# A two-layer decoder trunk on one core: one rank for all work, half-size weight parts in the mixers, and two of four weight sums of an FFN block made by an ACT copy and an accumulating DMA

## The chip, the cores and the metric

The kernel runs on one core of a Trainium2 chip. The metric is device time in microseconds (us) of one execution; lower is better. The engines are named as in the profile: PE (matrix multiplications; PEld is its weight load), DVE, ACT, POOL, and SP, which issues most loads.

## The reference, cut to what matters

The reference runs 256 positions of width 2048 through two layers in float32. Layer 0 mixes with a state-space part and a latent attention, layer 1 with a stick-breaking attention; each mixer is followed by a gated feed-forward network (FFN) of hidden width 5632.

```python
for layer in range(DEPTH):                      # DEPTH = 2
    h = rms_norm(x, mix_norm[layer])
    mix = ssd_mla_mixer(h, ...) if layer % 2 == 0 else stick_breaking_mixer(h, w_qkv[o], w_out_odd[o])
    x = x + mix
    x = x + swiglu_ffn(rms_norm(x, ffn_norm[layer]), w_gate[layer], w_up[layer], w_down[layer])
return rms_norm(x, final_norm)

def swiglu_ffn(h, w_gate, w_up, w_down):
    return (jax.nn.silu(h @ w_gate) * (h @ w_up)) @ w_down
```

## The kernel before, in words

**Products.** Every float32 weight is split into two parts that PE takes at full rate: `split` (L247) lets ACT copy the tile `w` into a rounded high part `wh` (L249), and DVE subtracts it from `w` to give the low part `wl` (L250). The activations are split the same way. A product is then three matmuls: high by high, low by high, high by low. Weights are loaded by SP in tiles of 128 partitions x 4 x 512 floats (1 MB), called `w`. There are four of them in turn during an FFN and three elsewhere; `wh` and `wl` have three each during an FFN and two elsewhere (`wtile`, L102). The fourth and the third lie in a shared pool that `region` (L88) opens and closes with each stage.

**Projections.** `project` (L333) computes 512 output columns for both halves of the positions: for each of 16 (or 8, or 12) k tiles of 128 rows it issues six matmuls (L340 to L342), so that one weight tile of four k feeds 24 matmuls. `load_split` (L300) loads and splits the weights. After each k tile `tick` (L81) moves a count of units on and lets waiting pieces of side work (transposes, attention, norms) issue their instructions.

**FFN blocks.** `ffn` (L550) goes through 11 blocks of 512 hidden columns in groups of 2, 2, 2, 2 and 3. A block is `pair` (L467): it computes gate and up together. For the first half of the contraction it takes seven products of 512 x 512 in place of eight, after the manner of Strassen: of the tiles b11 (gate), b12 (up), b22 (up) and b21 (gate) it forms t1 = b11 + b12, t2 = t1 + b22, t4 = t2 + b21 and t3 = b12 + b22 on DVE (`wadd`, L461, run at L464), splits seven tiles (b11, b22, t1, b21, t2, t4, t3, in that order of use) and runs 12 matmuls for each (L493, L494, L498). The second half is done plainly: four tiles called `cl`, 24 matmuls for each (L526 to L528). At its end `left` and `right` (L558, L559, L564, L566) make the hidden block h, which is transposed by PE within the next block, two units after its start. After each group a down projection by `project` follows: 8 or 12 weight tiles, each pair of output tiles added to the residual x by `add_residual` (L390, run on DVE at L395). PE transposes the new x for the next stage (L259, L413).

**What sets the order.** PE's instructions stand in the order in which the code is written. On every other engine and queue a scheduler puts the instructions in an order of its own when the program is built: of what is ready it takes the one with the lowest priority number. At run time each engine keeps strictly to that order. Weight work has numbers that count up from 100000 (`self.wprio`, +1000 for a projection's tile, +100 for each step of a block); side work that names nothing has 10000000, that is, after all weight work that is ready; what is marked `URGENT` has 50000.

Of the kernel before, what the change touches and what calls it, by code (L numbers as in the profile page):

```python
# [27 lines left out]
class Trunk:  # L28
# [6 lines left out]
    def __init__(self, ctx, tc, ins, out):  # L35
        self.tc, self.nc, self.i, self.out = tc, tc.nc, ins, out
        ec = ctx.enter_context
        self.cp = ec(tc.tile_pool(name="const", bufs=1))
        self.wp = ec(tc.tile_pool(name="weights", bufs=4))
        self.ap = ec(tc.tile_pool(name="acts", bufs=42))  # L40
        self.sp = ec(tc.tile_pool(name="small", bufs=2))
        ps = bass.MemoryType.PSUM
        self.pacc = ec(tc.tile_pool(name="pacc", bufs=1, space=ps))
        self.ptr = ec(tc.tile_pool(name="ptr", bufs=4, space=ps))
        self.dp = ec(tc.tile_pool(name="scratch", bufs=1, space=bass.MemoryType.DRAM))
        self.shared, self.shared_kind = None, None
# [3 lines left out]
        self.n, self.wn = 0, {}  # L50
        self.now, self.tasks = 0, []
        self.wprio = 100000
        tc.cur_priority = 10000000

    @contextmanager
    def priority(self, at):

        keep, self.tc.cur_priority = self.tc.cur_priority, at
        yield
        self.tc.cur_priority = keep  # L60


    def spawn(self, gen):
# [16 lines left out]

    def tick(self):  # L81
        self.now += 1
        ready = [t for t in self.tasks if t["wake"] <= self.now]
        for t in ready[:2]:
            if not t["done"]:
                self.advance(t)

    def region(self, kind):  # L88

        if self.shared is not None:  # L90
            self.shared.__exit__(None, None, None)
        self.shared, self.shared_kind = None, kind
        if kind:
            bufs = 20 if kind == "acts" else 2
            self.shared = self.tc.tile_pool(name=f"shared_{kind}", bufs=bufs, reuse_waits="tile")
# [12 lines left out]

    def whtile(self):
        return self.wtile("wh", F32R, 3, 2)  # L110

    def wltile(self):
        return self.wtile("wl", F32R, 3, 2)

    def wsum(self):
        return self.xp.tile([P, 4, 512], F32, name=self.nm("wsum"), tag="wsum", bufs=2)
# [25 lines left out]
    def constants(self):  # L142
# [4 lines left out]
        with self.priority(0):  # L147
            nc.sync.dma_start(rows_m, i["mix_norm"].rearrange("l (k p) -> (l k) p", p=P))
        for j in range(4):
            with self.priority(self.wprio + 1000 * j - 500):  # L150
                nc.sync.dma_start(self.xres[:, :, j * 512:(j + 1) * 512],
                                  i["x"][0, :, j * 512:(j + 1) * 512].rearrange("(t p) d -> p t d", p=P))
        with self.priority(self.wprio + 3500):
            self.small_loads(rows_a, rows_b)
        with self.priority(self.wprio + 6500):
# [144 lines left out]
    def load_split(self, view, nk, n):  # L300

        nc = self.nc
        for k0 in range(0, nk, 4):
            k1 = min(nk, k0 + 4)
            res = []
            with self.priority(self.wprio):
                self.wprio += 1000
                w = self.wtile()
                for dst, src in view(w, k0, k1):
                    nc.sync.dma_start(dst, src)  # L310
                order = ExitStack()
                for ins in self.first if self.wprio <= 105000 else ():
                    order.enter_context(self.tc.issue_after(ins))
                wh, wl = self.whtile(), self.wltile()
                step = 1 if self.wprio < 102000 else 2 if self.wprio < 106000 else k1 - k0
                for c in range(0, k1 - k0, step):
                    d = c + step
                    self.split(wh[:, c:d, :n], wl[:, c:d, :n], w[:, c:d, :n])
                order.close()
                for k in range(k0, k1):  # L320
                    res.append((wh[:, k - k0, :n], wl[:, k - k0, :n]))
            yield from res

    @staticmethod
# [65 lines left out]
    def add_residual(self, ps, j, scale=None):  # L390
        nc, x = self.nc, self.xres
        for t in range(2):
            xs = x[:, t, j * 512:(j + 1) * 512]
            if scale is None:
                nc.vector.tensor_tensor(xs, ps[t], xs, op=ALU.add)  # L395
            else:
                nc.vector.scalar_tensor_tensor(xs, ps[t], scale[:, t:t + 1], xs, op0=ALU.mult, op1=ALU.add)


    URGENT = 50000  # L400
# [42 lines left out]
            res.append((hi, lo))  # L443
        return res

    def wload(self, view, k0):
        w = self.wtile()
        with self.priority(self.wprio):
            self.wprio += 100
# [4 lines left out]
    def wsplit(self, w):  # L454
        wh, wl = self.whtile(), self.wltile()
        with self.priority(self.wprio):
            self.wprio += 100
            self.split(wh, wl, w)
        return wh, wl

    def wadd(self, o, p, q):  # L461
        with self.priority(self.wprio):
            self.wprio += 100
            self.nc.vector.tensor_tensor(o, p, q, op=ALU.add)  # L464
        return o

    def pair(self, st, xT, va, vb, left, right):  # L467
# [11 lines left out]
        w22 = self.wsplit(b22)  # L479
        wt1 = self.wsplit(t1)  # L480
        t4 = self.wadd(self.wsum(), t2, b21)
        w21 = self.wsplit(b21)
        wt2, wt4, wt3 = self.wsplit(t2), self.wsplit(t4), self.wsplit(t3)
        self.join(st["xT"][0][0])
        self.join(st["xT"][1][0])
        z, p3, p2, p4 = self.banks
# [42 lines left out]
        for half in range(2):  # L529
            k0, last = 8 + 4 * half, half == 1  # L530
            for side in range(2):
                wh, wl = self.wsplit(cl[half][side])
# [593 lines left out]
```

## Time and profile before

| | before |
|---|---|
| median of 3 runs | 2513.11 us (2512.77 to 2513.15) |
| profiled execution, its own time | 2512.09 us |
| its span in the trace | 2510.4 us |
| mean granted PE clock | 0.991 |
| PE, DVE, ACT, POOL busy | 98%, 68%, 52%, 5% of the span |
| read from HBM | 450.85 MB, 180 GB/s over the span |

The profiled execution is 1.7 us longer than its span, and 1.0 us under the median. The first mixer fills the first 641 us of the span, FFN 0 runs to about 1320 us, the second mixer to 1779 us, FFN 1 to the end. Busy shares are averages over these stages; a wait counts only where it ends last.

### The profile page before, as it was taken

The numbers are of one execution on the slowest core, as the hardware profiler recorded it, in microseconds if no ns is written. First come the engines' busy times: TensorE is split into PE (matmuls) and PEld (weight loads), VectorE is DVE, ScalarE is ACT, GpSimd is POOL, SyncE is SP. The second block draws the span as 40 slices with busy tenths as digits, with TensorE's granted clock in tenths as the row PEclk, the third lists the DMA queues.
The fourth block names the chain that finished last, engine by engine and source line by source line (L and its number), as shares of the span: only waits on it lengthen the run. The fifth ranks groups of instructions, "written<-read, shape, count | busy, mean of one in ns | idle before, by whom it ended". The sixth has DMA issues, their size and how long they took to land.

```text
span 2510.4 us, 27612 instructions
## 1 busy us (share of the span) xinstructions
PE 2454.1 (98%) x11176; PEld 2008.4 (80%) x11176; DVE 1714.3 (68%) x1476; ACT 1298.1 (52%) x1266; POOL 130.9 (5%) x164
## 2 busy tenths in 40 slices
PE   8999999999899999999999999999899999999998
PEld 7788877788688888888878787778688888888876
DVE  5775455456778778787965444445787878787874
ACT  6655555434554545454544545554554545454553
POOL 1231121000000000000000000000000000000001
PEclk9999999999899999999999999999999999999999
DMA  7654553355555556565554454445555656565653
GB/s 234 194 176 159 178 157 111 126 193 185 182 197 199 194 196 206 184 203 185 204 190 143 166 172 160 151 155 173 181 200 184 217 172 215 170 231 168 235 188 114
DMA packets 257824, 454.78 MB, mean 181 GB/s; under 512 B 20716, under 2 KB 45424, under 8 KB 257696
## 3 DMA queue, kind: packets, MB, share of 16 engines
q1 hardware_dynamic: 255168, 446.48, 53.1%
q0 software_dynamic: 1952, 5.48, 0.6%
q8 instruction: 88, 1.44, 0.2%
q10 hardware_dynamic: 576, 1.05, 0.1%
q14 instruction: 40, 0.33, 0.0%
HBM read 450.85 MB, written 2.13 MB: 180 GB/s over the span
## 4 chain that ended last, share of the span: by engine, by line
PE 56%; issue 39%; ACT 2%; DVE 1%; POOL 0%; DMA 0%; SPq 0%; POOLq 0%; ACTq 0%; DVEq 0%
PE acc L341 11%; PE acc L340 11%; PE acc L342 11%; PE acc L527 3%; PE acc L526 3%; PE acc L528 3%; PE acc L493 3%; PE acc L494 3%; PE acc L498 3%; PE tr L259 1%; ACT wh L249 1%; DVE wl L250 1%; PE at L1049 1%; PE at L978 1%; PE at L1048 0%
## 5 line engine op out<-in xcount | busy, mean ns | idle before, releaser
L250 DVE TENSOR_TENSOR wl<-w,wh 128x2048 fp32r<-128x2048 f32 (+2 forms) x431 | 966.3, 2250 | 578.3 <-ACT wh L249 569.5
L249 ACT CAST wh<-w 128x2048 fp32r<-128x2048 f32 (+2 forms) x431 | 807.3, 1875 | 732.5 <-PE acc L342 414.8
L340 PE MATMUL acc<-wh,s 128*128 128x512 f32 (+1 forms) x1728 | 692.2, 401 | 3.3 <-ACT wh L249 3.3
L341 PE MATMUL acc<-wl,s 128*128 128x512 f32 (+1 forms) x1728 | 673.6, 390 | 7.0 <-DVE wl L250 6.9
L342 PE MATMUL acc<-wh,s 128*128 128x512 f32 (+1 forms) x1728 | 674.2, 390 | 0.0
L341 PEld LDWEIGHTS acc<-wl,s 128*128 128x128 f32 x1728 | 326.2, 189 | 74.4 <-DVE wl L250 10.3
L342 PEld LDWEIGHTS acc<-wh,s 128*128 128x128 f32 x1728 | 325.3, 188 | 70.2
L340 PEld LDWEIGHTS acc<-wh,s 128*128 128x128 f32 x1728 | 325.9, 189 | 67.6 <-ACT wh L249 4.1
L528 PE MATMUL acc<-wl,s 128*128 128x512 f32 x704 | 275.3, 391 | 0.0
L527 PE MATMUL acc<-wh,s 128*128 128x512 f32 x704 | 275.2, 391 | 0.0
L526 PE MATMUL acc<-wh,s 128*128 128x512 f32 x704 | 275.2, 391 | 0.0
L493 PE MATMUL acc<-wh,s 128*128 128x512 f32 x616 | 246.4, 400 | 0.0
L494 PE MATMUL acc<-wh,s 128*128 128x512 f32 x616 | 242.4, 393 | 0.0
L249 ACT CAST wh<-wsum 128x2048 fp32r<-128x2048 f32 x66 | 125.9, 1910 | 84.6 <-PE acc L527 35.7
L498 PE MATMUL acc<-wl,s 128*128 128x512 f32 x616 | 166.1, 391 | 0.0
L250 DVE TENSOR_TENSOR wl<-wsum,wh 128x2048 fp32r<-128x2048 f32 x66 | 150.6, 2285 | 13.8 <-ACT wh L249 13.8
L527 PEld LDWEIGHTS acc<-wh,s 128*128 128x128 f32 x704 | 132.2, 188 | 29.1
L526 PEld LDWEIGHTS acc<-wh,s 128*128 128x128 f32 x704 | 132.2, 188 | 29.0
L528 PEld LDWEIGHTS acc<-wl,s 128*128 128x128 f32 x704 | 132.1, 188 | 29.0
L493 PEld LDWEIGHTS acc<-wh,s 128*128 128x128 f32 x616 | 116.9, 190 | 25.6
L494 PEld LDWEIGHTS acc<-wh,s 128*128 128x128 f32 x616 | 117.0, 190 | 24.3
L498 PEld LDWEIGHTS acc<-wl,s 128*128 128x128 f32 x616 | 115.8, 188 | 25.7
(246 smaller groups left out, 2063.3 us busy)
## 6 DMA issues: line engine op xcount, KB each, us to landing
w<-in_w_gate_dram SPq DMA_DIRECT2D x88, 1024.0 KB, 5.1
w<-in_w_up_dram SPq DMA_DIRECT2D x88, 1024.0 KB, 5.1
w<-in_w_down_dram SPq DMA_DIRECT2D x88, 1024.0 KB, 5.0
w<-in_w_qkv_dram SPq DMA_DIRECT2D x48, 1024.0 KB, 5.0
w<-in_w_in_dram SPq DMA_DIRECT2D x47, 1024.0 KB, 5.2
w<-in_w_out_even_dram SPq DMA_DIRECT2D x32, 1024.0 KB, 4.9
w<-in_w_out_odd_dram SPq DMA_DIRECT2D x16, 1024.0 KB, 5.0
w<-in_w_ukv_dram SPq DMA_DIRECT2D x32, 256.0 KB, 4.1
```

Source lines behind the costliest of these rows:

```text
L249: nc.scalar.copy(hi, src)
L250: nc.vector.tensor_tensor(lo, src, hi.bitcast(F32), op=ALU.subtract)
L259: self.nc.tensor.transpose(pt[:, k, t * P:(t + 1) * P], src(t, 2 * k2 + k), self.ident)
L340: nc.tensor.matmul(ps[t], hi[:, ts], wh, start=k == 0, stop=False)
L341: nc.tensor.matmul(ps[t], hi[:, ts], wl, start=False, stop=False)
L342: nc.tensor.matmul(ps[t], lo[:, ts], wh, start=False, stop=k == nk - 1)
L493: mm(ps, hi[:, k], wh[:, k], start=start and k == 0, stop=False, skip_group_check=True)
L494: mm(ps, lo[:, k], wh[:, k], start=False, stop=False, skip_group_check=True)
L498: mm(ps, hi[:, k], wl[:, k], start=False, stop=k == 3, skip_group_check=True)
L526: mm(ps, hi, wh, start=False, stop=False, skip_group_check=True)
L527: mm(ps, lo, wh, start=False, stop=False, skip_group_check=True)
L528: mm(ps, hi, wl, start=False, stop=stop, skip_group_check=True)
```

## The change

1. **One rank.** `due(units)` gives a priority of 100000 + 250 times the unit at which something is needed. Weights get `due(0)` at the point of the program that uses them, and within a block 0, 2, 4 ... 26 units for its steps. Side work gets `due(4)` at each `tick`, so that it stands four units behind the weights of the same place and no longer behind all of them. `add_residual` becomes `URGENT`.
2. **Half-size parts in the mixers.** `wh` and `wl` come from `part`: in the mixers four buffers of two k tiles in place of two of four, in the FFNs three of four as before; all of them lie in the shared pool now. A 1 MB tile `w` is split there by two pairs of instructions.
3. **Two sums by DMA.** b12 is no longer loaded as a tile. t1 is made by an ACT copy of b11 into `wsum` and a DMA on POOL's queue that loads b12 and adds it to what stands there; t3 is made the same way from b22 in a `w` tile. t2 and t4 stay on DVE. A block loads seven tiles on SP and two by accumulating DMAs on POOL, where it loaded eight on SP.

```diff
+    def due(self, units):
+        return self.base + 250 * (self.now + units)
...
     def tick(self):
         self.now += 1
+        self.tc.cur_priority = self.due(self.SLACK)
...
-    def wtile(self, tag="w", dt=F32, bufs=4, own=3):
-        n = self.wn[tag] = self.wn.get(tag, 0) + 1
-        if self.shared_kind == "sums" and n % bufs == 0:
-            return self.xp.tile([P, 4, 512], dt, name=self.nm(tag), tag=tag, bufs=1)
-        return self.wp.tile([P, 4, 512], dt, name=self.nm(tag), tag=tag, bufs=own)
...
+    def wtile(self):
+        self.wn += 1
+        pool, bufs = (self.xp, 1) if self.shared_kind == "sums" and self.wn % 4 == 0 else (self.wp, 3)
+        return pool.tile([P, 4, 512], F32, name=self.nm("w"), tag="w", bufs=bufs)
+    def part(self, tag):
+        nk, bufs = (2, 4) if self.shared_kind == "acts" else (4, 3)
+        return self.xp.tile([P, nk, 512], F32R, name=self.nm(tag), tag=tag, bufs=bufs)
...
-            with self.priority(self.wprio):
-                self.wprio += 1000
+            with self.priority(self.due(0)):
                 w = self.wtile()
...
+                np = 2 if self.shared_kind == "acts" else 4
+                for a in range(k0, k1, np):
+                    b = min(k1, a + np)
+                    wh, wl = self.part("wh"), self.part("wl")
...
             xs = x[:, t, j * 512:(j + 1) * 512]
-            if scale is None:
-                nc.vector.tensor_tensor(xs, ps[t], xs, op=ALU.add)
...
+            with self.priority(self.URGENT):
+                if scale is None:
+                    nc.vector.tensor_tensor(xs, ps[t], xs, op=ALU.add)
...
+    def wcopy_add(self, o, p, view, k0, at):
+        with self.priority(self.due(at)):
+            self.nc.scalar.copy(o, p)
+            for dst, src in view(o, k0, k0 + 4):
+                self.nc.gpsimd.dma_start(dst, src, accum_op=ALU.add)
+        return o
...
-        b11, b12 = self.wload(va, 0), self.wload(vb, 0)
-        b22, b21 = self.wload(vb, 4), self.wload(va, 4)
-        cl = [(self.wload(va, 8), self.wload(vb, 8)), (self.wload(va, 12), self.wload(vb, 12))]
-        t1 = self.wadd(self.wsum(), b11, b12)
-        w11 = self.wsplit(b11)
-        t2 = self.wadd(self.wsum(), t1, b22)
-        t3 = self.wadd(b12, b12, b22)
...
+        b11, b22, b21 = (self.wload(*a) for a in ((va, 0, 0), (vb, 4, 2), (va, 4, 6)))
+        t1 = self.wcopy_add(self.wsum(), b11, vb, 0, 0)
+        t3 = self.wcopy_add(self.wtile(), b22, vb, 0, 2)
+        cl = [(self.wload(va, 8, 14), self.wload(vb, 8, 18)), (self.wload(va, 12, 22), self.wload(vb, 12, 26))]
+        w11, w22 = self.wsplit(b11, 0), self.wsplit(b22, 2)
+        wt1 = self.wsplit(t1, 4)
+        w21 = self.wsplit(b21, 6)
+        t2 = self.wadd(self.wsum(), t1, b22, 8)
+        wt2 = self.wsplit(t2, 8)
+        wt4 = self.wsplit(self.wadd(self.wsum(), t2, b21, 10), 10)
+        wt3 = self.wsplit(t3, 12)
```

PE's order is the same, instruction by instruction. The changed file has lines of its own: L250 becomes L255, L395 becomes L403, L464 becomes L477, L558 becomes L570, L566 becomes L578, the ACT copy is L470 and the accumulating DMA L472. Three places show how the order moves on the other engines.

**First place: DVE where the first mixer ends and FFN 0 begins.** `xres` is the residual x; the two rows on it add the last projection's two results, after which PE transposes x. Before, where `wsum_920` is t1, `wsum_923` t2, `w_913` t3 and `wsum_928` t4:

```order
L250 TENSOR_TENSOR wl_922_5152<-w_912_5133,wh_921_5151 128x2048
L395 TENSOR_TENSOR xres_80<-acc_878_4941,xres_80 128x512
L464 TENSOR_TENSOR wsum_920_5149<-w_912_5133,w_913_5135 128x2048
L250 TENSOR_TENSOR wl_925_5159<-w_914_5137,wh_924_5158 128x2048
L464 TENSOR_TENSOR wsum_923_5155<-wsum_920_5149,w_914_5137 128x2048
L464 TENSOR_TENSOR w_913_5135<-w_913_5135,w_914_5137 128x2048
L250 TENSOR_TENSOR wl_927_5163<-wsum_920_5149,wh_926_5162 128x2048
L395 TENSOR_TENSOR xres_80<-acc_879_4942,xres_80 128x512
```

The same place in the change, where `wsum_1107` is t1 (copied by ACT, then added to by the DMA), `w_1105` is b22 and `wsum_1121` is t2:

```order
L403 TENSOR_TENSOR xres_80<-acc_1062_5299,xres_80 128x512
L403 TENSOR_TENSOR xres_80<-acc_1063_5300,xres_80 128x512
L255 TENSOR_TENSOR wl_1114_5528<-w_1104_5507,wh_1113_5527 128x2048
L477 TENSOR_TENSOR wsum_1121_5543<-wsum_1107_5513,w_1105_5509 128x2048
L255 TENSOR_TENSOR wl_1116_5532<-w_1105_5509,wh_1115_5531 128x2048
L255 TENSOR_TENSOR wl_1118_5536<-wsum_1107_5513,wh_1117_5535 128x2048
L275 SCALAR_TENSOR_TENSOR s2_1094_5475<-tr_1092_5469,va_142,s2_1093_5474 128x256 x2
```

The five weight operations between the two adds are gone from there. The sum t2, which reads what the DMA writes, now stands ahead of the low part of b22, the tile of the second product.

**Second place: DVE across the seam of two neighbouring blocks in FFN 0.** The first row is the last `cl` tile of a block, the first L477 the next block's t2; L570, L576 and L578 finish the first block's h. The change:

```order
L255 TENSOR_TENSOR wl_1144_5746<-w_1112_5525,wh_1143_5745 128x2048
L477 TENSOR_TENSOR wsum_1162_5812<-wsum_1148_5782,w_1146_5778 128x2048
L570 TENSOR_TENSOR s2_1133_5575<-acc_1131_5561,s2_1133_5575 128x512
L255 TENSOR_TENSOR wl_1155_5797<-w_1145_5776,wh_1154_5796 128x2048
L570 TENSOR_TENSOR s2_1136_5654<-acc_1132_5562,s2_1136_5654 128x512
L255 TENSOR_TENSOR wl_1157_5801<-w_1146_5778,wh_1156_5800 128x2048
L578 SCALAR_TENSOR_TENSOR s2_1136_5654<-acc_1129_5559,rstd_1103_5499,s2_1136_5654 128x512
L576 TENSOR_TENSOR s2_1135_5628<-acc_1130_5560,s2_1135_5628 128x512
L578 SCALAR_TENSOR_TENSOR s2_1133_5575<-s2_1135_5628,rstd_1103_5499,s2_1133_5575 128x512
L255 TENSOR_TENSOR wl_1159_5805<-wsum_1148_5782,wh_1158_5804 128x2048
```

Before, three sums (L464) stood among these rows; now one does, and everything below it waits for the DMA that makes t1.

**Third place: ACT in the second mixer, at the logarithms of a group's attention.** L699 before and L711 in the change are the logarithms, with the load of their table ahead; `wh_1810` before and `wh_2050`, `wh_2052` in the change are the high part of the same weight tile. Before:

```order
L249 CAST wh_1798_10768<-w_1797_10766 128x2048
L688 ACTIVATE s2_1784_10704<-at_1783_10701 128x384
L691 ACTIVATE s2_1785_10705<-s2_1784_10704 128x384
L692 ACTIVATE s2_1785_10705<-s2_1785_10705 128x384
L699 ACT_TABLE_LOAD
L699 ACTIVATE s2_1776_10654<-s2_1776_10654 128x384
L699 ACTIVATE s2_1779_10671<-s2_1779_10671 128x384
L699 ACTIVATE s2_1782_10688<-s2_1782_10688 128x384
L249 CAST s2_1789_10738<-s2_1776_10654 128x384
L699 ACTIVATE s2_1785_10705<-s2_1785_10705 128x384
L249 CAST s2_1791_10744<-s2_1779_10671 128x384
L249 CAST wh_1810_10815<-w_1809_10813 128x2048
```

The change:

```order
L711 ACT_TABLE_LOAD
L711 ACTIVATE s2_2012_11127<-s2_2012_11127 128x384
L711 ACTIVATE s2_2015_11144<-s2_2015_11144 128x384
L711 ACTIVATE s2_2018_11161<-s2_2018_11161 128x384
L254 CAST s2_2027_11215<-s2_2012_11127 128x384
L711 ACTIVATE s2_2021_11178<-s2_2021_11178 128x384
L254 CAST s2_2029_11221<-s2_2015_11144 128x384
L254 CAST wh_2050_11296<-w_2049_11294 128x1024
L254 CAST s2_2031_11227<-s2_2018_11161 128x384
L254 CAST wh_2052_11300<-w_2049_11294 128x1024
```

The weight tile stands in the same place, but its first half is a row of half the size.

More of the change, by code (lines that the diff above doesn't have):

```diff
@@ L93, in region @@
         if kind:
-            bufs = 20 if kind == "acts" else 2
-            self.shared = self.tc.tile_pool(name=f"shared_{kind}", bufs=bufs, reuse_waits="tile")
+            self.shared = self.tc.tile_pool(name=f"shared_{kind}", bufs=2, reuse_waits="tile")
             self.xp = self.shared.__enter__()
@@ L311, in load_split @@
                 order = ExitStack()
-                for ins in self.first if self.wprio <= 105000 else ():
+                for ins in self.first if self.now < 16 else ():
                     order.enter_context(self.tc.issue_after(ins))
[L314 to L318, printed above, removed]
+                np = 2 if self.shared_kind == "acts" else 4
+                for a in range(k0, k1, np):
+                    b = min(k1, a + np)
+                    wh, wl = self.part("wh"), self.part("wl")
+                    step = 1 if self.now < 4 else np
+                    for c in range(0, b - a, step):
+                        d = min(c + step, b - a)
+                        self.split(wh[:, c:d, :n], wl[:, c:d, :n], w[:, a - k0 + c:a - k0 + d, :n])
+                    for k in range(a, b):
+                        res.append((wh[:, k - a, :n], wl[:, k - a, :n]))
                 order.close()
-                for k in range(k0, k1):
-                    res.append((wh[:, k - k0, :n], wl[:, k - k0, :n]))
             yield from res
@@ L452, in wload, with wsplit, wadd @@
         return w
[L454 to L457, printed above, removed]
+    def wsplit(self, w, at):
+        wh, wl = self.part("wh"), self.part("wl")
+        with self.priority(self.due(at)):
             self.split(wh, wl, w)
         return wh, wl
[L461 to L463 removed]
+    def wcopy_add(self, o, p, view, k0, at):
+        with self.priority(self.due(at)):
+            self.nc.scalar.copy(o, p)
+            for dst, src in view(o, k0, k0 + 4):
+                self.nc.gpsimd.dma_start(dst, src, accum_op=ALU.add)
+        return o
+    def wadd(self, o, p, q, at):
+        with self.priority(self.due(at)):
             self.nc.vector.tensor_tensor(o, p, q, op=ALU.add)
@@ L531, in pair @@
             for side in range(2):
-                wh, wl = self.wsplit(cl[half][side])
+                wh, wl = self.wsplit(cl[half][side], 0)
                 if not last:
```

28 lines of the change are left out of this document (9 added, 19 removed).

## Prediction

> **What bounds the kernel now.** I read the page's busy shares first, then the groups of PE's waits, then the timelines of PE and DVE around the longest of them.
>
> The page: busy time of each engine, and the chain that ended last, by engine:
>
> ```profile
> PE 2454.1 (98%) x11176; PEld 2008.4 (80%) x11176; DVE 1714.3 (68%) x1476; ACT 1298.1 (52%) x1266; POOL 130.9 (5%) x164
> PE 56%; issue 39%; ACT 2%; DVE 1%; POOL 0%; DMA 0%; SPq 0%; POOLq 0%; ACTq 0%; DVEq 0%
> ```
>
> PE is busy 2454.1 of 2510.4 us. Its matmuls are the same afterwards, in the same order, so at most the 56 us of gaps and some slow clock can be won. The gaps, by what PE waited for (total, times, longest), and the single waits that I use:
>
> ```profile
> PE tr L259 <- DVE xres L395: 22.7, 2, 11.4
> PE acc L341 <- DVE wl L250: 8.7, 6, 1.8
> PE acc L340 <- ACT wh L249: 4.3, 5, 1.1
> PE tr L259 <- DVE s L566: 4.3, 2, 2.2
> 327.04 0.50 PE L341 MATMUL acc<-wl,s 128*128 128x512 f32 x1 [1.22 <-DVE wl L250]
> 1440.53 0.50 PE L340 MATMUL acc<-wh,s 128*128 128x512 f32 x1 [0.65 <-ACT wh L249]
> 1442.85 0.79 PE L341 MATMUL acc<-wl,s 128*128 128x512 f32 x1 [1.82 <-DVE wl L250]
> 1520.43 0.49 PE L340 MATMUL acc<-wh,s 128*128 128x512 f32 x1 [1.01 <-ACT wh L249]
> 1522.76 0.50 PE L341 MATMUL acc<-wl,s 128*128 128x512 f32 x1 [1.83 <-DVE wl L250]
> 1679.20 0.50 PE L340 MATMUL acc<-wh,s2x 128*128 128x512 f32 x1 [1.05 <-ACT wh L249]
> 1681.53 0.80 PE L341 MATMUL acc<-wl,s2x 128*128 128x512 f32 x1 [1.82 <-DVE wl L250]
> ```
>
> Nearly all is in three kinds of place: two starts of an FFN (22.7), four places in the second mixer (three are shown, the fourth near 1600 is 1.05 + 1.82; together 11.05), and two blocks behind a down projection (4.3). Inside the blocks PE waits for nothing. Some of these waits are followed by a slow clock (start:end and length, busy times, then PEclk):
>
> ```profile
> 1256.25:1262.50 6.25, 5.26 (x20) 4.35 (x21) 6.25 (x6) 2.33 (x4) 0.00 (x0) 0.73 0.15 58
> 1600.00:1606.25 6.25, 4.94 (x16) 4.18 (x17) 4.99 (x6) 4.52 (x5) 0.00 (x0) 0.73 0.59 177
> ```
>
> A granted clock of 0.73 over 6.25 us costs 1.7 us, behind three of the mixer's four waits and one of the blocks'.
>
> **The unknown: X, from issue to landing of the 1 MB DMA that adds.** No row shows one. The nearest (KB, us to landing; then the load queue's packets, MB and share of 16 engines; then DVE's sum and ACT's copy of a tile):
>
> ```profile
> w<-in_w_up_dram SPq DMA_DIRECT2D x88, 1024.0 KB, 5.1
> s<-acs_rows POOLq DMA_DIRECT2D x16, 256.0 KB, 5.0
> q1 hardware_dynamic: 255168, 446.48, 53.1%
> L464 DVE TENSOR_TENSOR w<-w,w 128x2048 f32<-128x2048 f32 x22 | 50.2, 2282 | 0.0
> L249 ACT CAST wh<-w 128x2048 fp32r<-128x2048 f32 x415 | 792.7, 1910 | 725.0 <-PE acc L342 409.9 <-PE acc L527 119.3 <-DVE xres L395 66.0
> ```
>
> Below, X is the 5.1 of the same bytes from SP; above, 20, four times POOL's 256 KB at 5.0. Between: the load queue took 53.1% of 2510.4 us for 446.48 MB, which is 3.13 us for each 1.05 MB, so a plain 1 MB on POOL would be 5.0 + 0.75 x 3.13 = 7.3. If adding means reading the destination as well, another 3.13 makes 10.5. I take **X = 9.5**, between these two and nearer the second, since an addition must read what it adds to. This is an estimate.
>
> The Trainium skill's "Collectives: The Full Stack", section "Why ReduceScatter is half of AllGather", says that an addition inside a DMA costs no cycles but a second source read, which halves the rate. By it X is 10.5 and the time 2500 by the formula below; no run here shows it.
>
> **The change, part by part.** The sum is made against the profiled execution (2512.09 us; span 2510.4 and 1.7 around it), 1.0 under the median.
>
> *a. Second mixer.* At 1520 PE waits because ACT, held by the logarithms' table load and activations, casts the next weight tile late, and the subtraction follows. With halves, a slot of two k tiles, one of four, comes free 8.2 us (three halves) ahead of use, not one tile of 5.5 us (a product's pace in b, twice), and the first half needs about 1.05 and 1.22 us on ACT and DVE, not 1.91 and 2.29 (groups of 128x1024):
>
> ```profile
> L250 DVE TENSOR_TENSOR wl<-w,wh 128x1024 fp32r<-128x1024 f32 x12 | 14.4, 1220 | 5.3 <-ACT wh L249 5.2
> L249 ACT CAST wh<-w 128x1024 fp32r<-128x1024 f32 x12 | 12.3, 1051 | 7.5 <-PE acc L342 5.0 <-DMA w<-in_w_ukv_dram 1.5 <-DMA w<-in_w_in_dram 0.8
> ```
>
> So 2.7 us more of a lead and 0.9 + 1.1 us less work stand against waits of 2.5 to 2.9. I keep 0.3 for each: 11.05 + 3 x 1.7 - 1.2 = **-15**. The ends are 0 (the row on ACT stays as it is) and -16.2. The extra instructions (two for one, some 0.2 us each) lie where DVE and ACT are idle.
>
> *b. The two starts of an FFN.* PE's last matmul of the mixer, the transpose that waited, and the seventh product (672.27) and first plain tile (675.00); then DVE's row between the two additions to the residual:
>
> ```profile
> 640.71 0.40 PE L342 MATMUL acc<-wh,s2x 128*128 128x512 f32 x1
> 652.79 1.76 PE L259 MATMUL tr<-ident,xres 128*128 128x128 f32 x7 [11.28 <-DVE xres L395]
> 672.27 0.39 PE L493 MATMUL acc<-wh,s 128*128 128x512 f32 x1
> 675.00 0.39 PE L526 MATMUL acc<-wh,s 128*128 128x512 f32 x1
> ...
> 640.43 0.69 DVE L395 TENSOR_TENSOR xres<-acc,xres 128x512 f32<-128x512 f32 x1 [0.65 <-PE acc L342]
> 641.04 2.28 DVE L464 TENSOR_TENSOR wsum<-w,w 128x2048 f32<-128x2048 f32 x1
> 643.24 2.28 DVE L250 TENSOR_TENSOR wl<-w,wh 128x2048 fp32r<-128x2048 f32 x1
> 645.45 2.28 DVE L464 TENSOR_TENSOR wsum<-wsum,w 128x2048 f32<-128x2048 f32 x1
> 647.65 2.28 DVE L464 TENSOR_TENSOR w<-w,w 128x2048 f32<-128x2048 f32 x1
> 649.85 2.28 DVE L250 TENSOR_TENSOR wl<-wsum,wh 128x2048 fp32r<-128x2048 f32 x1
> 652.05 0.68 DVE L395 TENSOR_TENSOR xres<-acc,xres 128x512 f32<-128x512 f32 x1
> ```
>
> Five tile operations of 2.2 us hold the second addition back. `URGENT` brings it next to the first, and the wait of 11.3 goes. But t2 now stands on DVE ahead of w22's low part, and t2 needs the DMA. From 641.1 to 675.0 are 33.9 us. In the change ACT's copy of b11 waits for a slot of the last region; the DMA lands about X - 0.9 behind the mixer's last matmul. Then DVE does t2, w22's low, t1's low (6.6), four short gain rows (1.7), w21's low (10.6 in all), t2's low (13.0 with 0.2 for a hand-over), t4 (15.4), ACT casts t4 (17.3), DVE takes its low part (19.5), and PE has 0.9 + 2.7 + 0.4 left to the end of the seventh product: 23.5, thus X + 22.6. The gain is 11.3 - X at FFN 0. At FFN 1 the copy waits for a matmul 2.9 us later: 8.4 - X. Together 19.7 - 2X: **-0.7** at 9.5, ends -9.5 (X = 5.1) and +20.3 (X = 20).
>
> *c. The seams of blocks.* A product is 2.73 us (672.27 to 675.00), a plain tile 5.46, a block 41.0. In the block, the first `cl` tile's high part gets its slot among three late in the fifth product (12.7), then 1.9 on ACT, 2.2 on DVE: 16.8. That frees the buffer for the next b11: loaded by 21.9, copied by 23.8, t1 landed by 23.8 + X. On DVE, t2, two low parts, two L570, L578, L576, L578 (3 x 2.2 + 5 x 0.6 = 9.6) must then end before PE transposes h, at 41.0 + 2.73 = 43.7. So it holds while **X is under 10.3** at the ten second blocks of a group. In the two third blocks b11's buffer comes free some 1.5 later (my estimate from the order of rows there), which makes the limit 8.8: 0.7 each, **+1.4**. The eight behind a down projection hold to 11.6, and the two waits of L566 there (4.3, and 1.7 of clock) go, since only one of three sums stands in their row: **-6**. SP's eight loads become seven, and 44 sums of 2.28 us leave DVE for ACT, which is idle half the time: nothing by itself, as no PE wait in a block is for DVE's throughput.
>
> *d. The rest.* The wait at 327 goes to the halves: **-1.2**. At the second mixer's start the first half's low part now stands behind both urgent additions: **+1.6** (two of 0.68 and a hand-over).
>
> POOL issues 44 more DMAs; nothing else stands on its queue in the FFNs (0.00 in the window at 1256), so this costs what is in X.
>
> Sum at X = 9.5: -15 - 0.7 + 1.4 - 6 - 1.2 + 1.6 = -19.9. Span 2490.5, run 2492.2, median **2493**. With X left open it is -40.3 + 2X (X to 8.8), then also 2(X - 8.8) + 10(X - 10.3) + 8(X - 11.6), each term from its threshold, and 1.7 of slow clock for three in four of the waits over 1.8. X = 5.1 gives 2483, 7.3: 2487, 10.5: 2500, 11.2: 2513, 12: 2527, 13: 2561, 20: some 2720.
>
> **Rivals.** *Fast DMA.* X is 5 to 8.5: 2483 to 2490. For it speaks that SP moves the same bytes in 5.1, against it that POOL's plain loads took 5.0 for a quarter of them.
>
> *DVE stands at t2.* The DMA lands late, and the one instruction that reads it holds up the finishing of h behind it, 20 times. It decides from X = 11.2; at 13 the time is 2561, **slower than before**. For it: any second packet cost per row of 2 KB, or POOL's own time per descriptor, comes 44 times 512 rows. Against it: 16 issues on POOL while DVE was busy 77% took 536 to 572 ns each:
>
> ```profile
> L944 POOL DMA_DIRECT2D s<-acs_rows x16: 536/538/572, 92.0 to 175.6; - x16
> 100.00:200.00 100.00, 99.92 (x504) 82.01 (x504) 77.23 (x143) 63.04 (x70) 40.53 (x35) 1.00 0.54 180
> ```
>
> The Trainium skill's "SBUF — State Buffer", section "Who interferes with whom", warns that a DMA issued on POOL starves for descriptors while DVE holds the ports that they share, and advises SP's or ACT's queue. By that rule X would grow by up to a DVE operation, and this rival would win; the same page exempts the kind of subtraction that fills DVE here, and the even issues agree.
>
> *Ranks do nothing for the mixer.* The halves arrive no earlier, since ACT's row keeps the tile behind the logarithms: -15 becomes 0, and the time is 2508.
>
> *Near balance.* X of 10.9 to 11.7: 2508 to 2518.
>
> **Numbers.** Forecast (X 8.5 to 10.9) 0.33; fast DMA 0.17; no help in the mixer 0.05; balance 0.07; DVE stands 0.38. Under 0.2%, about what a measurement of this kernel can tell, counts as the same: 2508 to 2518. Faster is 0.33 + 0.17 + 0.03 = 0.53, same 0.07 + 0.02 = 0.09, slower 0.38. The range runs from 2478 to 2561. Its lower end is X = 5.1 with step a at its own end (1.2 more) and a clock that stays up at the starts, 1.8 us each by the row
>
> ```profile
> 650.00:656.25 6.25, 3.46 (x12) 3.08 (x13) 6.25 (x7) 2.51 (x7) 0.00 (x0) 0.50 0.50 168
> ```
>
> (3.46 us of matmuls at half speed). Above the upper end lies half of the slow rival, 0.19. The likeliest case alone has 2488 to 2508.
>
> **What would show it.** The accumulating DMAs' landing time is X itself. Step a: no PE waits on L347 or L348 in the second mixer. Step b: the transposes wait under 1 us for L403, and the products behind them wait for low parts instead. Step c: PE's waits for L578, and L477's idle time put down to a DMA. If X is over 11.2, or if PE waits inside blocks for low parts, the forecast is wrong.

## The result, and the profile after

The change makes the kernel slower: 2550.62 us median of 4 runs (2549.01 to 2552.36) against 2513.13 us before, a ratio of 1.0143 (95% interval 1.0125 to 1.0161). The profiled execution has a span of 2550.1 us, 39.7 more than before. The forecast was 2493; the measured time lies inside its range, on the other side of no change.

First the page of the change: busy time of each engine.

```profile
PE 2486.9 (98%) x11176; PEld 2006.9 (79%) x11176; DVE 1641.0 (64%) x1587; ACT 1396.9 (55%) x1465; POOL 186.0 (7%) x208
```

The reader is to see two things. PE has the same 11176 matmuls, but they take 2486.9 us where they took 2454.1: 32.8 of the 39.7 us are **busy** time (a matmul that runs slowly counts as busy). And DVE, which lost 44 sums, is no longer of interest: it fell by 73 us, and nothing came of it. Next, what PE waited for in the change (total, times, longest):

```profile
PE acc L505 <- ACT s L516: 23.1, 14, 2.3
PE acc L510 <- DVE wl L255: 11.2, 2, 5.9
PE tr L264 <- DVE s L578: 8.6, 10, 1.5
...
PE acc L348 <- DVE wl L255: 1.8, 2, 1.7
PE tr L264 <- DVE xres L403: 0.7, 2, 0.4
PE at L982 <- POOL s L979: 0.6, 1, 0.6
PE acc L347 <- ACT wh L254: 0.6, 1, 0.6
```

The waits of the second mixer (L347, L348 now) are gone but for one, the waits for the residual fell from 22.7 to 0.7, and new ones stand in the FFNs: for a copy by ACT (L516), for low parts at the two starts (L510), for the block's h (L578). Then the accumulating DMAs' issues in the change (KB, median us to landing):

```profile
wsum<-in_w_up_dram POOLq DMA_DIRECT2D x22, 1024.0 KB, 8.7
w<-in_w_up_dram POOLq DMA_DIRECT2D x22, 1024.0 KB, 8.6
```

and, by their line, how long an issue holds POOL (ns: least, median, most):

```profile
L472 POOL DMA_DIRECT2D wsum<-in_w_up_dram x22: 1273/1282/1356, 642.8 to 2411.4; - x22
```

X, the unknown of the prediction, is 8.7 us in the median: under the 9.5 that was taken, and far under the 11.2 from which it was to decide the sign. One by one, the DMAs for t1, on which h waits, took 8.4 to 10.5; only the two for t3 at the starts of the FFNs took 13.

Because PE's order is the same in both kernels, the two traces can be laid side by side matmul by matmul. Worked out from them: the time from the start of each matmul to the next, summed by stage, as change minus before. "Pace" sums the pairs whose distances differ by no more than 16 ns; "rest" is what waits and slow clock add or take. (FFN 0 ends at 1368 us of the span before, later than the table of before has it.)

```
stage           before   change   difference   of it pace   rest   forecast
first mixer      638.1    640.6      +2.5         +5.3      -2.8     -1.2
start of FFN 0    34.3     33.9      -0.4         +0.3      -0.7  \  -0.7
start of FFN 1    33.7     36.5      +2.9         +0.2      +2.6  /
FFN 0            692.7    716.2     +23.4        +11.0     +12.5  \  -4.6
FFN 1            688.6    713.2     +24.6        +11.2     +13.3  /
second mixer     411.1    398.0     -13.1         +3.3     -16.4    -13.4
sum                                 +39.8        +31.3      +8.5    -19.9
```

So the mixer did what was forecast. Two things did not: in every stage most matmuls of the change are a little slower, and the FFNs lose 26 us in waits where they should have won 5.

**The pace, seen in rows.** Here are the first matmuls of two neighbouring plain tiles of FFN 1, 24 matmuls apart, in the timeline of before:

```profile
1818.06 0.39 PE L526 MATMUL acc<-wh,s 128*128 128x512 f32 x1
...
1823.51 0.39 PE L526 MATMUL acc<-wh,s 128*128 128x512 f32 x1
```

and the same two in the change:

```profile
1833.33 0.40 PE L538 MATMUL acc<-wh,s 128*128 128x512 f32 x1
...
1838.93 0.40 PE L538 MATMUL acc<-wh,s 128*128 128x512 f32 x1
```

5.45 us became 5.60, without a wait between them and at a granted clock of 1.00. The view of PE's waits shows nothing of it.

**The seam of two blocks, seen in rows.** In the change, at the first seam of FFN 0, by ACT, POOL, DVE, ACT again, and PE:

```profile
682.00 1.91 ACT L470 COPY wsum<-w 128x2048 f32<-128x2048 f32 x1 [3.29 <-DMA w<-in_w_gate_dram]
...
684.20 1.28 POOL L472 DMA_DIRECT2D wsum<-in_w_up_dram  x1 [36.46 <-ACT wsum L470]
...
692.62 2.29 DVE L477 TENSOR_TENSOR wsum<-wsum,w 128x2048 f32<-128x2048 f32 x1 [4.59 <-DMA wsum<-in_w_up_dram]
...
705.66 1.91 ACT L254 CAST wh<-wsum 128x2048 fp32r<-128x2048 f32 x1 [1.71 <-PE acc L506]
707.47 0.58 ACT L516 COPY s<-acc 128x512 f32<-128x512 f32 x1
...
699.45 0.39 PE L505 MATMUL acc<-wh,s 128*128 128x512 f32 x1
...
702.70 0.63 PE L264 MATMUL tr<-ident,s 128*128 128x128 f32 x4 [0.29 <-DVE s L578]
...
708.10 0.50 PE L505 MATMUL acc<-wh,s 128*128 128x512 f32 x1 [1.54 <-ACT s L516]
```

The chain that the prediction wrote down is there: copy, DMA, t2 on DVE, which stands idle 4.59 us for the DMA, then h, which PE awaits for 0.29 us (the second block's first matmul is the row at 699.45). But PE's larger loss comes after it. L516 copies the result of the first product out of z (the accumulator that four of the seven products share), so that the third product may go on in z. In ACT's row it stands behind the cast of t2, and that cast waits for a slot that the second product frees (705.66). The copy is `URGENT`, yet the row is fixed when the program is built. PE stands 1.54 us.

### The profile page after: what moved, and what is told of

The parts are those of the page before. It is cut to its first block, busy times and chain, and to the rows that moved or that the text cites. A ratio compares the mean times of both kernels' runs of the same rounds, so it can differ in the third digit from the quotient of the medians.

```text
span 2550.1 us, 28145 instructions
## 1 busy us (share of the span) xinstructions
PE 2486.9 (98%) x11176; PEld 2006.9 (79%) x11176; DVE 1641.0 (64%) x1587; ACT 1396.9 (55%) x1465; POOL 186.0 (7%) x208
## 3 DMA queue, kind: packets, MB, share of 16 engines
q0 software_dynamic: 25184, 51.62, 11.2%
## 4 chain that ended last, share of the span: by engine, by line
PE 58%; issue 31%; DMA 4%; DVE 4%; ACT 2%; POOL 1%; POOLq 0%; SPq 0%; DVEq 0%; ACTq 0%
PE acc L347 12%; PE acc L348 12%; PE acc L349 12%; DMA wsum<-in_w_up_dram 4%; PE acc L540 4%; PE acc L538 4%; PE acc L539 4%; PE acc L505 3%; PE acc L506 3%; PE acc L510 2%; DVE wl L255 2%; PE tr L264 1%; ACT wh L254 1%; DVE s L578 1%; PE at L990 1%
## 5 line engine op out<-in xcount | busy, mean ns | idle before, releaser
L255 DVE TENSOR_TENSOR wl<-w,wh 128x1024 fp32r<-128x1024 f32 (+2 forms) x586 | 1000.5, 1713 | 614.7 <-ACT wh L254 612.4
L254 ACT CAST wh<-w 128x1024 fp32r<-128x1024 f32 (+2 forms) x586 | 832.8, 1425 | 692.3 <-PE acc L349 402.4
L347 PE MATMUL acc<-wh,s 128*128 128x512 f32 (+1 forms) x1728 | 696.9, 403 | 0.6 <-ACT wh L254 0.6
L348 PE MATMUL acc<-wl,s 128*128 128x512 f32 (+1 forms) x1728 | 679.2, 393 | 1.8 <-DVE wl L255 1.8
L349 PEld LDWEIGHTS acc<-wh,s 128*128 128x128 f32 x1728 | 325.1, 188 | 75.9
L348 PEld LDWEIGHTS acc<-wl,s 128*128 128x128 f32 x1728 | 326.0, 189 | 72.9 <-DVE wl L255 2.8
L347 PEld LDWEIGHTS acc<-wh,s 128*128 128x128 f32 x1728 | 325.8, 189 | 70.5 <-issue 1.4
L540 PE MATMUL acc<-wl,s 128*128 128x512 f32 x704 | 278.0, 395 | 0.0
L539 PE MATMUL acc<-wh,s 128*128 128x512 f32 x704 | 278.0, 395 | 0.0
L538 PE MATMUL acc<-wh,s 128*128 128x512 f32 x704 | 277.9, 395 | 0.0
L505 PE MATMUL acc<-wh,s 128*128 128x512 f32 x616 | 250.7, 407 | 25.1 <-ACT s L516 23.1
L506 PE MATMUL acc<-wh,s 128*128 128x512 f32 x616 | 244.9, 398 | 0.0
L510 PE MATMUL acc<-wl,s 128*128 128x512 f32 x616 | 172.2, 402 | 11.2 <-DVE wl L255 11.2
L477 DVE TENSOR_TENSOR wsum<-wsum,w 128x2048 f32<-128x2048 f32 x44 | 100.6, 2287 | 112.2 <-DMA wsum<-in_w_up_dram 112.2
L505 PEld LDWEIGHTS acc<-wh,s 128*128 128x128 f32 x616 | 117.3, 190 | 59.8 <-ACT s L516 29.8
L539 PEld LDWEIGHTS acc<-wh,s 128*128 128x128 f32 x704 | 132.3, 188 | 31.7
L538 PEld LDWEIGHTS acc<-wh,s 128*128 128x128 f32 x704 | 132.4, 188 | 31.6
L255 DVE TENSOR_TENSOR wl<-wsum,wh 128x2048 fp32r<-128x2048 f32 x66 | 149.9, 2284 | 7.4 <-ACT wh L254 7.4
L510 PEld LDWEIGHTS acc<-wl,s 128*128 128x128 f32 x616 | 118.1, 192 | 40.4 <-DVE wl L255 12.1
```

The lines of the kernel that those rows point to most:

```text
L254: nc.scalar.copy(hi, src)
L255: nc.vector.tensor_tensor(lo, src, hi.bitcast(F32), op=ALU.subtract)
L347: nc.tensor.matmul(ps[t], hi[:, ts], wh, start=k == 0, stop=False)
L348: nc.tensor.matmul(ps[t], hi[:, ts], wl, start=False, stop=False)
L349: nc.tensor.matmul(ps[t], lo[:, ts], wh, start=False, stop=k == nk - 1)
L505: mm(ps, hi[:, k], wh[:, k], start=start and k == 0, stop=False, skip_group_check=True)
```

## The experiments

Two theories were set against each other. **P**: PE's pace depends on where the weight parts lie in memory, and they moved (the change puts all of `wh` and `wl` in the shared pool). **Q**: the adding DMAs, or more traffic, slow PE's reads. In the compiled programs each address of the change's shared pool is 448 modulo 2048 and each address of the activations `s` is 832. Before, two of three `wh` and `wl` were at 832 as well. The activations called `s2x` lie in the shared pool in both kernels. Grouped by the difference of the two addresses, the matmuls into `acc` (distance to the next start, those under 260 ns) are:

```
kernel                                 weights minus activations, modulo 256: matmuls, mean ns
before                                 0: 6667, 226.3    128: 2733, 232.7
the change                             0:  731, 227.2    128: 8640, 231.8
e1 (the change, 384 bytes)             0: 9333, 226.3
e2 (the change, 128 bytes)             0: 9356, 226.4
e3 (before, 384 bytes)                 0: 9410, 226.3
e12 (before, 64 bytes)                 0: 6657, 226.3    64: 730, 229.1    192: 2015, 233.3
```

The 731 in the change are those between two tiles of the shared pool, `s2x` and a weight part: both lie at 448, and they keep the good pace to within a nanosecond. So the distance of the two counts, and not the place. The last four lines come from the experiments. An unused tile ahead of the shared pool moves the addresses and nothing else; all instructions keep their order:

```diff
-        self.sp = ec(tc.tile_pool(name="small", bufs=2))
+        self.sp = ec(tc.tile_pool(name="small", bufs=2)); ec(tc.tile_pool(name="pad", bufs=1)).tile([P, 96], F32, name="pad")
```

**e1, the change with 384 bytes.** 

> The changed kernel with an unused tile of 384 bytes in front of the shared pool: every instruction and its order stay, only the addresses of wh, wl, wsum, s2x and the fourth w move up by 384, so that they agree with the activations' modulo 2048. Theory P (the pace of a matmul depends on how its weight tile and its activation tile lie to each other): about 8200 matmuls go from 232.9 to 227.4 ns, -45 us, some 2506 us. Rival Q (the pace is slower because the adding DMAs, or more traffic in all, disturb PE's reads): no change, 2550 us.

Measured: 2534.88 us (ratio to before 1.0088, 1.0071 to 1.0106). PE's busy time in the padded change:

```profile
PE 2454.1 (97%) x11176; PEld 2015.7 (79%) x11176; DVE 1640.4 (65%) x1587; ACT 1396.6 (55%) x1465; POOL 185.8 (7%) x208
```

PE's waits in the same kernel:

```profile
PE tr L264 <- DVE s L578: 28.3, 12, 3.7
PE acc L505 <- ACT s L516: 22.8, 14, 2.3
PE acc L510 <- DVE wl L255: 11.6, 2, 6.3
```

The pace is back to the last matmul, as P says. Laid beside the change as in the table by stage, it gives back 48.3 us, more than the 31.3 that the change had lost, because the 2733 matmuls that were slow before are mended too. (That PE's busy time is again the 2454.1 of before is chance.) But the time falls by 16 us only, not 45: the waits for h grow from 8.6 to 28.3, and the clock, which was granted at half for 34.1 us of the span in the change, is at half for 61.8. X has hardly moved (9.0 and 8.7 us):

```profile
wsum<-in_w_up_dram POOLq DMA_DIRECT2D x22, 1024.0 KB, 9.0
w<-in_w_up_dram POOLq DMA_DIRECT2D x22, 1024.0 KB, 8.7
```

So a slow PE had given the DMA chain time; a faster one waits for it.

**e2, the change with 128 bytes.** 

> The same with 128 bytes, so that the two differ by 256 modulo 2048. Theory P with agreement needed modulo 256 or less: as with 384 bytes, about 2506 us. Theory P with agreement needed modulo 512 or more: as without padding, about 2550 us. Rival Q: 2550 us.

Measured: 2534.16 us (1.0089, 1.0062 to 1.0115), the same as e1. It is enough that the addresses agree modulo 256.

**e3, before with 384 bytes.** 

> The kernel before with the same 384 bytes; nothing else. Theory P: its third wh and wl and its s2x tiles, about 2700 matmuls at 5.3 ns too much, gain 14 us: 2499 us. Rival Q: 2513 us.

Measured: 2494.25 us (0.9927, 0.9907 to 0.9946): some 19 us faster than before by a tile that nobody reads. The kernel before had the same fault for a third of its weight parts. Q falls: there is no adding DMA here.

**e12, before with 64 bytes.** 

> The kernel before with 64 bytes of padding, so that the shared pool's tiles differ from the activations' by 64 modulo 256 (without padding by 128, with 384 bytes by 0). If only a difference of 128 is bad: as with 384 bytes, about 2494 us. If every difference but 0 is bad: matmuls between the two keep a mean of some 232 ns and the time is 2510 to 2515 us.

Measured: 2511.36 us (0.9994, 0.9985 to 1.0004). Differences of 64 and 192 are slow too, the table above shows by how much (64 occurs only with `s2x`, in 730 matmuls); of those tried, only 0 is good.

**e4, all sums on DVE again, no padding.** The wait for X goes, ranks and halves stay:

```diff
-        t1 = self.wcopy_add(self.wsum(), b11, vb, 0, 0)
-        t3 = self.wcopy_add(self.wtile(), b22, vb, 0, 2)
+        b11, b12, b22, b21 = (self.wload(*a) for a in ((va, 0, 0), (vb, 0, 1), (vb, 4, 2), (va, 4, 6)))
...
+        t1 = self.wadd(self.wsum(), b11, b12, 4)
...
+        t3 = self.wadd(b12, b12, b22, 8)
```

> The changed kernel with all four sums on DVE again and b12 loaded as a tile: ranks and halves remain, no adding DMA. Theory P: the slow pace stays (PE's busy time within 5 us of the change's 2486.9), and only the waits at the starts and seams (some 40 us in all) can go: 2515 to 2535 us. Rival Q: the pace is that of before, 2505 us or less.

Measured: 2536.61 us (1.0094, 1.0079 to 1.0109), with PE busy 2491.2 us. The pace stays slow without any adding DMA: Q falls again. The time lies just above what was expected. By stage, against the change, the starts win 8.0 us and the FFNs only 6.4: besides pace, the FFNs still take 19.6 us more than in the kernel before, without an adding DMA.

**e7, e4 with 384 bytes.** 

> The change with all sums on DVE and 384 bytes of padding: ranks and halves alone, at the good pace. If pace and adding DMAs are two causes that add up: 2536.6 - 47 (8640 matmuls at 5.5 ns) = 2490, at most 2498 with waits that grow. If the ranks themselves spoil the seams, as a third cause: above 2505 us.

Measured: 2492.64 us (0.9925, 0.9910 to 0.9940). With pace and adding DMAs both taken away, the loss is gone. But against the padded before (e3) ranks and halves win almost nothing, 1.6 us: by stage they give 13.8 in the second mixer and 5.5 at the starts, and lose 18.2 in the FFNs (696.4 + 693.5 against 688.1 + 683.6), where PE waits for casts, h and low parts (of the first line two waits, 9.3 us, stand at the starts, and two of the third, 2.9):

```profile
PE acc L505 <- ACT wh L254: 12.7, 10, 4.8
PE tr L264 <- DVE s L578: 10.4, 7, 2.6
PE acc L510 <- DVE wl L255: 4.5, 10, 1.6
```

**e8, what X is made of.** The padded change with plain loads over the copy; the addition is left out, so t1 and t3 are both just b12:

```diff
-                self.nc.gpsimd.dma_start(dst, src, accum_op=ALU.add)
+                self.nc.gpsimd.dma_start(dst, src)
```

> The padded change with both DMAs on POOL as plain loads over the copy, which leaves the addition out (t1 is b12, t3 is b12). If the addition costs X its second read: X falls from 9.0 to about 6 us, the waits of L578 (28.3 us) shrink by some 20, and the time is near 2510 us. If X is POOL's descriptors and queue: X stays within 0.5 us of 9 and the time at 2535 us.

Measured: 2494.39 us (0.9926, 0.9910 to 0.9943), 40.5 us under e1. The DMAs of this kernel:

```profile
wsum<-in_w_up_dram POOLq DMA_DIRECT2D x22, 1024.0 KB, 6.3
w<-in_w_up_dram POOLq DMA_DIRECT2D x22, 1024.0 KB, 5.7
```

their issue on POOL:

```profile
L472 POOL DMA_DIRECT2D wsum<-in_w_up_dram x22: 748/748/789, 636.5 to 2356.5; - x22
```

and PE's waits:

```profile
PE acc L505 <- ACT s L516: 25.2, 14, 3.2
PE acc L510 <- DVE wl L255: 5.6, 2, 3.1
PE tr L264 <- DVE s L578: 5.2, 4, 1.7
```

In e1 the two DMAs took 9.0 and 8.7 us, so the addition costs 2.7 to 3.0 us, and the issue is 0.53 us longer with it (1282 against 748 ns). It decides over the waits for h (28.3 against 5.2) and half of those at the starts (11.6 against 5.6), and leaves those for L516 alone. The time fell further than expected, since the slow clock that follows the waits went as well (23.8 us at half, from 61.8).

**e5, the copy of z first.** The padded change, with the casts of t2, t4 and t3 written behind the first copy of z and tied behind it on ACT:

```diff
-        wt2 = self.wsplit(t2, 8)
-        wt4 = self.wsplit(self.wadd(self.wsum(), t2, b21, 10), 10)
-        wt3 = self.wsplit(t3, 12)
+        t4 = self.wadd(self.wsum(), t2, b21, 10)
...
         z1 = keep()
+        with self.tc.issue_after(self.kept):
+            wt2 = self.wsplit(t2, 6)
+            wt4 = self.wsplit(t4, 8)
+            wt3 = self.wsplit(t3, 10)
```

> The padded change (384 bytes, 2534.9 us), with the casts of t2, t4 and t3 written behind the first copy of z and tied behind it on ACT, so that this copy no longer waits for a cast. Theory S (the copy's 14 waits, 22.8 us in the padded change, are a loss of their own): they go and the time falls by 15 to 23 us, to 2512 to 2520 us. Rival T (the seam is bound by the adding DMA and DVE's row behind it, and the copy's wait only stands where another would): the time stays above 2528 us and the waits for low parts or for h grow by what the copy's waits lose.

Measured: 2517.82 us (1.0022, 1.0010 to 1.0033), 17.1 us under e1. The waits for the copy fall from 22.8 to 2.7 us, those for h grow by 3.6 only: theory S.

```profile
PE tr L264 <- DVE s L580: 31.9, 12, 3.3
PE acc L503 <- ACT s L514: 2.7, 8, 0.4
```

**e11, t2 behind h as well.** On top of e5:

```diff
-        t2 = self.wadd(self.wsum(), t1, b22, 8)
+        with self.tc.issue_after(self.hlast) if self.hlast else ExitStack():
+            t2 = self.wadd(self.wsum(), t1, b22, 8)
```

> The padded change with the first copy of z ahead of t2's cast (2517.8 us), and t2's sum tied on DVE behind the last row of the last block's h. Rival 'DVE stands at t2' in its pure form: the 31.9 us of waits for h go and nothing takes their place, 2485 to 2495 us with the adding DMAs kept. If t2, t4 and t3 are late themselves: waits for low parts of t2 or t1 take their place, 2505 us or more.

Measured: 2502.46 us (0.9956, 0.9940 to 0.9973), between the two expectations. The waits for h are gone; waits for casts and low parts in the products (L504, L509 there; 2.0 and 12.2 us of them stood in e5 already) take some seven tenths of their place:

```profile
PE acc L504 <- ACT wh L254: 20.4, 11, 2.0
PE acc L509 <- DVE wl L255: 16.2, 14, 6.3
```

So t2's other place in DVE's row wins 15.4 us, but the tiles themselves are late too: with the adding DMAs kept and both rows mended, the kernel is still 10 us behind e7.

**e6, step b alone.** The padded before, with the additions to the residual `URGENT`, as the change has them. 

> The padded kernel before (2494.3 us), with the additions to the residual marked URGENT and nothing else. Forecast of step b (the wait of 11.3 us at each FFN's start is DVE's five tile operations between the two additions): most of 22.6 us goes, 2475 to 2482 us. Rival: the same five operations are needed by the first products, PE waits for their low parts instead, and the time stays within 5 us of 2494.

Measured: 2496.8 us (0.9943, 0.9928 to 0.9958), against 2494.25 for the padded before: nothing. PE's waits show why (its lines are one higher than those of before: L505 is the copy of z, L494 a product):

```profile
PE acc L494 <- ACT s L505: 18.9, 6, 4.6
```

The 22.6 us of waits for the residual are gone, and 18.9 us of waits for ACT's copy of z have come instead. The rival was right about the time, though it named another wait. All four sums stay on DVE here, as they did before, so this tells what `URGENT` does alone, not what it does once t1 and t3 are made elsewhere.

**e9, step a by instructions alone.** The padded before; in the mixers each tile is split by two pairs of instructions, in the same two slots of four k tiles:

```diff
-                step = 1 if self.wprio < 102000 else 2 if self.wprio < 106000 else k1 - k0
+                step = 1 if self.wprio < 102000 else 2 if self.wprio < 106000 or self.shared_kind == "acts" else k1 - k0
```

> The padded kernel before (2494.3 us), with each weight tile of the mixers split by two pairs of instructions in the same two slots. If step a's gain comes from shorter instructions: the second mixer gets 7 or more of the 13.8 us that it loses from the padded before to the padded change, 2487 us or less. If it comes from the four slots of two k tiles: under 4 us, 2491 us or more.

Measured: **2480.74 us (0.9870, 0.9855 to 0.9885), the fastest kernel of the study.** The second mixer falls from 406.4 to 391.5 us. Of PE's waits for weight parts one is left:

```profile
PE tr L259 <- DVE xres L395: 22.6, 2, 11.4
PE tr L259 <- DVE s L566: 6.9, 6, 2.6
...
PE acc L340 <- ACT wh L249: 0.7, 1, 0.7
```

**e10, step a by slots.** The padded before, with `wh` and `wl` of the mixers in four slots of two k tiles in the shared pool, ranks and FFNs as before. 

> The padded kernel before with step a alone: wh and wl of the mixers in four slots of two k tiles, ranks and FFNs as before. If the halves alone make step a: the second mixer falls by 13 us and the time is 2478 to 2483 us, the fastest of all. If the ranks made it: 2490 us or more.

Measured: 2497.76 us (0.9932, 0.9917 to 0.9947). The second mixer falls as much as expected (393.0 us), but the first one rises from 636.0 to 650.3, with new waits for POOL; in e7, with the change's ranks, it takes 634.9. So without the ranks the four slots hurt the first mixer. Which of its many small rows they hold up was not traced.

```profile
PE at L971 <- POOL s L968: 10.1, 3, 3.4
```

## Why the prediction was wrong, point by point

- **What bounds the kernel.** "Its matmuls are the same afterwards, in the same order, so at most the 56 us of gaps and some slow clock can be won" holds for what can be won. The sum then treated PE's busy time as fixed also against losses. That is the step that failed first: the pace cost +31.3 us, a term that was not in the sum. The sentence on the change said that the parts now lie in the shared pool; what that does to PE was not asked. The trace of before, read with the addresses of its tiles, would have shown it: its matmuls fall into two groups, 226.3 and 232.7 ns. Alone, however, this term does not make the whole loss: with the pace mended in the change (e1) the time falls by 16 us, since the seams then take the rest.
- **X.** Taken as 9.5, measured 8.7. Its two parts were both a little high: a plain load 5.7 to 6.3 (taken 7.3), the addition 2.7 to 3.0 (bound by 3.13). For the addition of a collective, the Trainium skill's "Collectives: The Full Stack" gives a second source read as the reason in "Why ReduceScatter is half of AllGather". The 2.7 to 3.0 measured are near the 3.13 at which a second read was put, which agrees with that in size; the X of 10.5 that the prediction worked out by it was not reached, because the plain load was shorter than taken. (At X of 10.5, 11.2 and 12 the formula gives 2499, 2512 and 2526, each one less than what stands there; nothing hangs on it.)
- **Step a, second mixer: right in size, wrong in reason.** Forecast -13.4 with the part of d, measured -16.4 besides pace. The reason given first, slots that come free 8.2 us ahead, is not needed: two short instructions for a long one, in the old slots, give all of it (e9). The wait forecast at the start of the second mixer (d, 1.6) came too: 1.7 us, the longer one on L348.
- **Step b, starts: forecast -0.7, measured +1.9 besides pace.** t2 did stand on DVE ahead of w22's low part, and L510 waited for it, 11.2 us in the two. With X at 8.7 the step's own formula, 19.7 - 2X, wins 2.3, so the miss is 4.2. Here the copy of z was missing: PE waited 2.3 us for it at each start, and with the copy first (e5) the two starts take 2.1 and 1.9 less than in e1. e6 does not test the formula, since its sums stay on DVE; it shows that `URGENT` by itself gains nothing.
- **Step c, seams: forecast -4.6, measured +25.8 besides pace.** This failed in three places. The chain was right in its links, but not in its limit of 10.3: at the first seam b11 landed at 682.00, 17.4 us ahead of the next block's first matmul (699.45), where the working had 41.0 - 21.9 = 19.1, and PE waited 0.3 us for h at an X of 8.4 (684.20 to 692.62), so the limit was near 8. And it followed only DVE's row to h. ACT's row, where PE waited 1.5 us at each of 12 seams for the copy of z behind t2's cast, was not followed; that is 18.4 us in the FFNs. The other 4.7 of the 23.1 are the two starts, where short rows on x stand between that cast and the copy. Beyond this, the sum put the new ranks at nothing in the blocks: e4 has no adding DMA and no wait for the copy at the seams, and still loses 19.6 us besides pace in the FFNs, in other waits, most of them shorter. Of the 25.8, then, taking the adding DMAs away wins 6.4 only; which of the new ranks makes the other loss was not tried.
- **The rival "DVE stands at t2"** has the sign, and its 2561 us is near the time, but the change is not that rival: X stayed under its deciding point of 11.2, and in the change the waits for h are 8.6 us. Only once the pace is mended do they become 28.3. Its doubt about POOL's own time per descriptor is answered: 1282 ns for an issue, 1356 at most. The Trainium skill's rule on starved descriptors ("SBUF — State Buffer", "Who interferes with whom") would have shown in that spread, and does not, which agrees with its exemption of DVE's subtractions.

Together, from before by way of e3, e7 and e1 to the change: padding -19, ranks and halves -2, adding DMAs +42, padding taken away again +16, which makes +37. In the other order, without padding, ranks, halves and moved parts cost 23 and the adding DMAs 14. The DMAs' price is three times as high when PE runs at its good pace.

## What to carry to other kernels

When a tile moves to another pool, ask where it lies as well as when it comes: compare the distances between matmuls that wait for nothing, tile by tile, before treating PE's busy time as given. When an engine's row is fixed at build time, follow each row that the critical engine waits for, and look in it for a short, urgent instruction behind a long one that waits. And before a term is added to a sum, ask whether the gain would be seen: a wait that goes at one place (e6), or a pace that is mended (e1), gave a wait to the next link.

## What the runs showed of the hardware

- Start to start, 128x512 matmuls took 226.3 ns in the mean where the streamed weight part and the activations loaded into PE lay at addresses equal modulo 256 (in one partition), and 229 to 233 ns at differences of 64, 128 and 192. Some 2700 of 9400 matmuls at the slower pace cost the kernel before some 19 us. Why the addresses matter was not tried; it is shown only that moving them, and nothing else, changes the pace.
- By the medians of each run, a 1 MB DMA on POOL that adds to its destination landed in 8.6 to 9.1 us (t3's in e11: 11.0), the plain one of e8 in 5.7 to 6.3, a plain one on SP in the FFNs in 5.0 to 6.0. The issue of the adding one held POOL 1282 ns, that of the plain one 748.
